# The recurrence over the context moved between the decays of later pieces, the later recurrence given precedence

## The chip, the cores and the metric

The kernel runs on one core of a Trainium2 chip. The metric is the device time of one launch in microseconds: for the kernel before, the median of 3 runs is 1711.6 (1711.44 to 1716.66). The engines are named as the profile does: PE (matrix products), PEld (loading of its weights), DVE (VectorE), ACT (ScalarE), POOL (GpSimd) and SP (the queue that issues the DMAs).

## The reference

One layer of a diffusion backbone, 1024 latent rows and 256 context rows of 1024 columns. Cut to what matters here:

```python
h  = modulate(rms_norm(x, norm1_g), shift, scale)        # the same for the context rows
cb, cc, cx, r, k, v, w_lo, a_lo, g_lo = split(h @ w_in)  # one input projection
def step(S, inp):                                        # a 64x64 state per head, 8 heads, two directions
    sa = einsum("bhvk,bhk->bhv", S, kk_t)
    S  = S * w_t - sa * b_t + v_t * k_t                  # w_t: the decay
    return S, einsum("bhvk,bhk->bhv", S, r_t)
ctx_state      = scan(step, zero, context rows)          # per direction
y              = scan(step, ctx_state, latent rows)      # starts from the context's last state
y_conv         = cb * shortconv1d(cc * cx, conv_a_w)
x = x + g1 * (concat(y_conv, rwkv_output(y, r, k, v, g_lo)) @ w_out)
x = x + g2 * conv_ffn(modulate(rms_norm(x, norm2_g), ...))   # gated, 3x3 convolution, 2816 columns
return rms_norm(x, final_g)
```

## The kernel before, in words

The recurrence is computed in chunks of 64 rows. Inside a chunk its rows form a triangular system; the kernel builds its matrices from the decays, inverts them, and then steps the state from chunk to chunk with matrix products. All of it is float32; wide products take their operands split in a high and a low part and are three products each.

**Stages, in the order of the program.** Modulation and norm; projections of k and v; then, for five *pieces* of 256 rows (one of the context, `ti` = 0, and four of the latents in the order 2, 8, 4, 6), `decay_and_invert(ti)`: `decays` (L524) makes decays and chunk matrices for four column groups `j` and two directions `d`, and `invert` (L652) inverts the piece's triangular blocks, mostly by 60 small products and sums on DVE (`tmp`, `ti`, L670 and L672). Beside the pieces stand `r_and_gate` (r and gate projections) and `conv_group` (the three projections of the short convolution and its arithmetic on DVE, L832 to L840); their products are `pj`, L354. In the text a *unit* is one column group of one piece, so 20 units; its end is the last reading of its chunk products `px` by DVE (L603).

**The steps.** `steps` (L723) advances both directions by one chunk. A step's chain is: `ry` (what the chunk's own rows and the state S give, L752 and L760, PE), `rh` (a copy, ACT for one direction and DVE for the other, L762), `pu` (L771, PE), `vu` (L775, L777), `ps` (L783, PE), the sum into S (L786, DVE), and then the next step's L760. POOL scales S (L764) and a chunk's `car` (L650). For the latents come the chunk's outputs: products L792 and their copy or sum (L800, L802). After every part of the chain `fill(n)` hands out n pieces of other work from a list (`pend`): the product of the convolution group with the output weights (`pco`), and from round 10 on mixing (`mix`), output product (`outp`, `po`) and the feed-forward's input (`to_h2`). The table SL says how many pieces stand in each of the four gaps of a round.

There are four steps over the context and then 16 *rounds* (r0 to r15) over the latents: r0 to r3 need the pieces 2 and 8 only, r4 is the first that needs piece 6. Before, the context's steps stand after all five pieces; behind each of them two of the eight blocks of `w_out` are multiplied by the gate (`w_make`, L891 on DVE, L892 on ACT, L893 on POOL), loaded two at a time.

**What sets the order.** A scheduler lists each engine's instructions, by priority in program order and by a model of time of its own; an engine then works through its list in that order. Tiles of SBUF and the eight PSUM banks are handed out by pools: a tile waits until the tile that held its place is done with. `B1` gives the banks for the pieces: `px` three, `pj` two, `pl` (decays' small products) two, `pq` one, and `ry`, `pu` one of `px`'s.

Of the kernel before, what the change touches and what calls it, by code (L numbers as in the profile page):

```python
# [2 lines left out]

# [12 lines left out]
D = 1024  # L16
# [6 lines left out]
CH = 64  # L23
# [5 lines left out]
TAIL = {10: "m3 m4", 11: "o3 o4 h3 h4", 12: "m2 m5", 13: "o2 o5 h2 h5", 14: "m1 m6", 15: "o1 o6 h1 h6", 16: "m0 m7", 17: "o0 o7", 18: "h0 h7"}  # L29
SL = ((3, 2, 0, 2),) * 10 + ((0, 1, 3, 4),) + ((4, 4, 4, 6),) * 5  # L30
RC = 9
# [3 lines left out]
YT = 2  # L35
IB = 2
XB, XT = 2, 3
PADC, PADM = 88, 80
PN1 = (5,)
NA = 17  # L40
XO = "xx0300301131x123222x"
AE = (0, 1, 0, 1, 0, 0, 1, 0)
B1 = ((4, 5, 1), (2, 3), (6, 7), (0,), (1,))
B2 = ((2, 3), (1, 6))
# [43 lines left out]
def hybrid_kernel(  # L88
# [96 lines left out]
    md = ss_.enter_context(tc.tile_pool(name="md", bufs=1, side="left", reuse_waits="tile"))  # L185
    md.tile([128, PADM], F32, name="padm")
    hsr = md.tile([128, 4, 2], F32, name="hsr")
# [325 lines left out]
    st = ss_.enter_context(tc.tile_pool(name="st", bufs=1, side="left", reuse_waits="tile"))  # L513
    sx = ExitStack()
    dq = sx.enter_context(tc.tile_pool(name="dq", bufs=2, side="left", reuse_waits="tile"))
    NP = 256
# [7 lines left out]
    def decays(pp, pieces):  # L524


        for ti in pieces:
# [4 lines left out]
            for j in range(4):  # L532
# [6 lines left out]
                if lat:  # L539
                    rt = dq.tile([128, NP], F32, name="dr")  # L540
                    SY.dma_start(rt, rd[j, :, t0 - CTX:t0 - CTX + n])
                    rk = dq.tile([128, NP], F32, name="rk", bufs=1)
                    G.tensor_tensor(out=rk, in0=rt, in1=k, op=ALU.mult)
                    pbn = pp.tile([128, 512], F32, name="pbn", tag="pl", bufs=2)
                    for q in range(2):
                        PE.matmul(pbn[:, 2 * q:2 * q + 2], rk[:, 128 * q:128 * q + 128], hsr[:, j, :], start=True, stop=True)
                    V.tensor_copy(bon[:, ti - 2:ti, 2 * j:2 * j + 2], pbn[:, 0:4].rearrange("p (t e) -> p t e", e=2))
# [70 lines left out]


    Sd = []  # L620
# [4 lines left out]
    zero = st.tile([128, 2], F32, name="zero")  # L625
    G.memset(zero, 0.0)
    yts, before = {}, [None, None]

    class Chunk:


        def __init__(self, pool, d, t, ch):
            self.d, self.t, self.ch, self.has_y = d, t, ch, t >= 2

            self.pc = before[d]
            before[d] = pcs[:, d, :, 2 * t + ch:2 * t + ch + 1]
            self.xa = pool.tile([128, 8, CH], F32, name="cxa")
            SY.dma_start(self.xa, xad[t // 2, :, ch, 2 * d + t % 2])
            self.kbt = pool.tile([128, 512], F32, name="ckb")
            SY.dma_start(self.kbt, kbd[d, t, ch])  # L640
            if self.has_y:
                self.ar = pool.tile([128, 4, 2 * CH], F32, name="car")
                SY.dma_start(self.ar, ard[d, t, ch])
                self.xr = pool.tile([128, 8, CH], F32, name="cxr")
                SY.dma_start(self.xr, xrd[d, t, ch])
            else:
                self.ar = pool.tile([128, 4, 2 * CH], F32, name="car")[:, :, 0:CH]
# [75 lines left out]
    def steps(pool, pairs, pp, bufs, sl=(0, 0, 0, 0)):  # L723


        cx = []
        rh = pool.tile([128, 512], F32, name="rh", bufs=1)
# [15 lines left out]
        rys = []  # L743
        for _ in cx:
            ry = pp.tile([128, 4, 128], F32, name="ry", tag="ry", bufs=bufs)
            rys.append((ry, ry.rearrange("p j (e v) -> p (j e) v", e=2)))
# [10 lines left out]
        for (u, v0, u0, vu, S), (ry, ry8) in both:  # L757
# [8 lines left out]
        pus = [pp.tile([128, 4, 128], F32, name="pu", tag="pu", bufs=bufs) for _ in cx]  # L766
        with turns():
# [4 lines left out]
        for (u, v0, u0, vu, S), pu in zip(cx, pus):  # L772
# [3 lines left out]
            else:  # L776
                chain["V"] = V.tensor_scalar(out=vu[u0:u0 + 64], in0=puf, scalar1=-1.0, scalar2=None, op0=ALU.mult)  # L777
        fill(sl[1])
        for u, v0, u0, vu, S in cx:

            ps = pp.tile([128, 4, 64], F32, name="ps", tag="pu", bufs=bufs)
            for h in range(8):
                chain["PE"] = PE.matmul(ps[64 * (h % 2):64 * (h % 2) + 64, h // 2, :], u.kbt[:, 64 * h:64 * h + 64], vu[:, 64 * h:64 * h + 64], start=True, stop=True)  # L783
            for e in range(2):
                r = slice(64 * e, 64 * e + 64)
                chain["V"] = V.tensor_tensor(out=S[r, :, r], in0=ps[r], in1=S[r, :, r], op=ALU.add)  # L786
        fill(sl[2])
        both = [z for z in both if z[0][0].has_y]
        with turns():
# [3 lines left out]
        for (u, v0, u0, vu, S), (ry, ry8) in both:  # L793
# [9 lines left out]
            e_[1] += 1  # L803
            if e_[1] == 2 and (first or t in (3, 4)):
                SY.dma_start(yd[t], e_[0])
        fill(sl[3])

# [36 lines left out]
    rg, cg = r_and_gate(), conv_group()  # L844

    def decay_and_invert(ti):
        for _ in decays(ppc, (ti,)):
            pass
        for _ in invert(ppc, ti):
            pass  # L850

    decay_and_invert(0)
    for _ in range(4):
        next(rg)
    for ti in (2, 8, 4, 6):
        decay_and_invert(ti)
# [11 lines left out]
    sh2 = ExitStack()  # L868
    h2p = sh2.enter_context(tc.tile_pool(name="h2p", bufs=1, side="left", reuse_waits="tile"))
    h2 = [[h2p.tile([128, 8, 512], F32R, name=f"h2{hf}{i}", tag=f"h2{hf}{i}") for i in range(2)] for hf in range(1)]  # L870

# [11 lines left out]
    def w_raw(k):  # L883
        raws_[k] = cp_.tile([128, D], F32, name="xo", bufs=XB)
        SY.dma_start(raws_[k], w_out[0, 128 * k:128 * k + 128, :])

    def w_make(k):
# [4 lines left out]
        A.copy(hl[0], raw)  # L892
        G.tensor_tensor(out=hl[1], in0=raw, in1=hl[0].bitcast(F32), op=ALU.subtract)  # L893

# [138 lines left out]
    stages = {"m": mix, "o": outp, "h": to_h2}  # L1033
    ppc = Banks(ry=B2[0], pu=B2[1])
    w_raw(0)
    w_raw(1)
    for r in range(4):
        steps(ring, [(0, r // 2, r % 2), (1, 1 - r // 2, 1 - r % 2)], ppc, 1)

        with behind():  # L1040
            w_make(2 * r)
            w_make(2 * r + 1)
        if r < 3:
            w_raw(2 * r + 2)
            w_raw(2 * r + 3)
        if r == 1:
            pend.append(conv_out())
            next(pend[0])
# [197 lines left out]
```

## Time and profile before

| | |
|---|---|
| median of 3 runs | 1711.6 us |
| the profiled execution | 1711.73 us, span 1710.0 us |
| PE busy | 1558.9 us (91%) |
| DVE busy | 1157.2 us (68%) |
| ACT, POOL busy | 565.1 (33%), 578.4 us (34%) |
| mean granted TensorE clock | 0.938 |

The busy share is an average over stages with different limits, so it is read stage by stage: which engine is busy there, and what ended its idle time. The pieces run from about 265 to 612 us, the context's steps from 617 us, the rounds until 938 us, the feed-forward from there to the end.

### The profile page before, as it was taken

Reading aid. Unit: us, or ns where it says so; the run is one execution under the profiler, and the core shown is the slowest. Engines: PE = TensorE matmul, PEld = TensorE weight load, DVE = VectorE, ACT = ScalarE, POOL = GpSimd, SP = SyncE. Lnnn points to the kernel's source line nnn. Section 1 sums busy time; section 2 is a strip of 40 time slices with the busy share of each in tenths; the row PEclk is TensorE's granted clock in tenths of the full one; section 3 lists DMA queues with packets and bytes.
Section 4 is the critical chain, followed back from the end, with each engine's and each line's share of the span. In section 5 each row is a group of like instructions: output and inputs, shape, how many; then the busy total and the mean of one; then the engine's idle time right before and its main releaser. Section 6 shows DMA issues by size and latency. Waiting matters only on the chain.

```text
span 1710.0 us, 27259 instructions
## 1 busy us (share of the span) xinstructions
PE 1558.9 (91%) x10639; PEld 1260.8 (74%) x10639; DVE 1157.2 (68%) x1795; ACT 565.1 (33%) x994; POOL 578.4 (34%) x515
## 2 busy tenths in 40 slices
PE   7699999989899966799678889999999999999997
PEld 2588768867777756687566768888888888788886
DVE  4963525698999987444578777777777777446645
ACT  2654315544445323221123421211111111324323
POOL 2343312333343304533344422222222222545643
PEclk9799799998999875999789999999999999999999
DMA  9385527557576486988652311111111111533531
GB/s 311 113 281 178 180 76 219 160 154 243 173 236 214 127 256 208 320 248 274 214 164 73 116 49 49 50 46 45 46 50 50 50 49 50 172 112 123 165 95 61
DMA packets 233721, 247.97 MB, mean 145 GB/s; under 512 B 18547, under 2 KB 171720, under 8 KB 233592
## 3 DMA queue, kind: packets, MB, share of 16 engines
q1 hardware_dynamic: 233208, 246.07, 46.2%
q8 instruction: 84, 1.38, 0.3%
q14 instruction: 45, 0.37, 0.1%
q0 software_dynamic: 384, 0.15, 0.0%
HBM read 179.32 MB, written 66.85 MB: 144 GB/s over the span
## 4 chain that ended last, share of the span: by engine, by line
PE 64%; DVE 23%; DMA 6%; ACT 3%; issue 3%; SPq 1%; POOL 0%; DVEq 0%; ACTq 0%
PE pf L1099 26%; PE pf L1179 13%; PE pj L354 10%; DVE tmp L670 3%; DVE ti L672 3%; PE pco L898 2%; PE po L898 2%; DMA araw<-in_ada_w_dram 2%; DVE acc L1146 2%; PE ry L760 1%; DVE xrO L605 1%; PE ry L752 1%; DVE xa L603 1%; PE ps L783 1%; PE px L601 1%
## 5 line engine op out<-in xcount | busy, mean ns | idle before, releaser
L1099 PE MATMUL pf<-h,fhi 128*128 128x512 f32 x1408 | 385.9, 391 | 5.9 <-DVE act L1151 4.1
L1099 PEld LDWEIGHTS pf<-h,fhi 128*128 128x128 f32 x1408 | 265.7, 189 | 62.6 <-DVE act L1151 4.5
L354 PE MATMUL pj<-hx,whi 128*128 128x512 f32 (+1 forms) x976 | 302.5, 389 | 1.6 <-DVE hx L328 1.3
L1146 DVE SCALAR_TENSOR_TENSOR acc<-gp,prm,acc 128x1024 f32<-128x1024 f32 x176 | 273.0, 1553 | 6.0
L106 POOL TENSOR_TENSOR flo<-fraw,fhi 128x1024 fp32r<-128x1024 f32 x50 | 122.0, 2441 | 315.8 <-ACT fhi L105 315.8
L1099 PE MATMUL pf<-h,flo 128*128 128x512 f32 x704 | 224.9, 392 | 0.0
L354 PEld LDWEIGHTS pj<-hx,whi 128*128 128x128 f32 x976 | 184.6, 197 | 38.2 <-issue 4.4
L354 PE MATMUL pj<-hx,wlo 128*128 128x512 f32 (+1 forms) x488 | 189.5, 389 | 0.0
L1179 PE MATMUL pf<-dhi,ahl 128*128 128x512 f32 x640 | 163.0, 389 | 0.2 <-DVE ahl L1171 0.2
L1171 DVE TENSOR_TENSOR ahl<-act,ahl 128x512 fp32r<-128x512 f32 x44 | 86.2, 1969 | 101.5 <-ACT ahl L1170 101.5
L1099 PEld LDWEIGHTS pf<-h,flo 128*128 128x128 f32 x704 | 132.9, 189 | 27.7 <-POOL flo L106 0.2
L105 ACT CAST fhi<-fraw 128x1024 fp32r<-128x1024 f32 x50 | 52.6, 1053 | 265.8 <-issue 158.4
L1179 PEld LDWEIGHTS pf<-dhi,ahl 128*128 128x128 f32 x640 | 120.0, 188 | 25.5 <-DVE ahl L1171 0.6
L106 POOL TENSOR_TENSOR dlo<-fraw,dhi 128x1024 fp32r<-128x1024 f32 x40 | 98.5, 2467 | 93.7 <-ACT dhi L105 89.7
L106 POOL TENSOR_TENSOR wlo<-wraw,whi 128x1024 fp32r<-128x1024 f32 x26 | 63.2, 2431 | 165.1 <-ACT whi L105 165.0
L1144 DVE TENSOR_SCALAR acc<-gp,prm 128x1024 f32<-128x1024 f32 x22 | 42.6, 1938 | 98.2 <-ACT gp L1136 98.2
L354 PEld LDWEIGHTS pj<-hx,wlo 128*128 128x128 f32 x488 | 96.2, 197 | 17.3 <-issue 1.7
L1179 PE MATMUL pf<-dlo,ahl 128*128 128x512 f32 x320 | 89.1, 389 | 0.0
L601 PE MATMUL px<-arO,kbO 64*128 64x128 f32 (+1 forms) x640 | 64.1, 308 | 18.3 <-DVE xrO L605 12.5
L601 PEld LDWEIGHTS px<-arO,kbO 64*128 64x128 f32 x640 | 51.9, 206 | 35.1 <-issue 29.2
L105 ACT CAST dhi<-fraw 128x1024 fp32r<-128x1024 f32 x40 | 41.9, 1050 | 105.0 <-PE pf L1179 87.5
L764 POOL TENSOR_TENSOR S<-S,pcs 128x512 f32<-128x512 f32 x38 | 40.1, 1069 | 94.1 <-PE ry L760 93.9
(281 smaller groups left out, 2621.6 us busy)
## 6 DMA issues: line engine op xcount, KB each, us to landing
araw<-in_ada_w_dram SPq DMA_DIRECT2D x48, 512.0 KB, 5.5
fraw<-in_ffn_w_up_dram SPq DMA_DIRECT2D x46, 512.0 KB, 3.9
fraw<-in_ffn_w_down_dram SPq DMA_DIRECT2D x44, 512.0 KB, 3.7
wraw<-in_w_in_dram SPq DMA_DIRECT2D x26, 512.0 KB, 5.3
lu<-lu_dram SPq DMA_DIRECT2D x20, 512.0 KB, 5.3
kb_dram<-kbT SPq DMA_DIRECT2D x40, 256.0 KB, 3.1
xa_dram<-xa SPq DMA_DIRECT2D x20, 512.0 KB, 4.9
cxa<-xa_dram SPq DMA_DIRECT2D x40, 256.0 KB, 3.8
```

The lines of the kernel that those rows point to most:

```text
L105: A.copy(hi, src)
L106: G.tensor_tensor(out=lo, in0=src, in1=hi.bitcast(F32), op=ALU.subtract)
L354: PE.matmul(p[:, :n], w[:, k, :], hsl(i, k, t0, n), start=(k == 0 and first), stop=(k == 7 and last))
L601: PE.matmul(px[:, ch, i, 0:w], kbO[r, i, 2 * ch:2 * ch + 2, :].rearrange("p s n -> p (s n)"), rhs, start=True, stop=True)
L670: V.tensor_tensor(out=tv, in0=ti[:, j + 1:32, j:j + 1].to_broadcast([128, m, j]), in1=ti[:, j:j + 1, 0:j].to_broadcast([128, m, j]), op=AL ...
L672: V.tensor_tensor(out=ti[:, j + 1:32, 0:j], in0=ti[:, j + 1:32, 0:j], in1=tv, op=ALU.add)
L898: m = PE.matmul(po, hl[:, a_, k, :], w[k][b_][:, sl], start=(k == 0 and f), stop=(k == 3 and l))
L1099: PE.matmul(pts[hf], w[:, k, :], h2[hf][i_][:, k, :], start=(k == 0 and f), stop=(k == 7 and l))
L1144: V.tensor_scalar(out=acc, in0=src, scalar1=wcol, scalar2=prm[:, P_FB + f:P_FB + f + 1], op0=ALU.mult, op1=ALU.add)
L1146: V.scalar_tensor_tensor(out=acc, in0=src, scalar=wcol, in1=acc, op0=ALU.mult, op1=ALU.add)
L1171: V.tensor_tensor(out=hl[:, 1, :], in0=asl, in1=hl[:, 0, :].bitcast(F32), op=ALU.subtract)
L1179: PE.matmul(pd[i], hl[:, a_, 128 * q:128 * q + 128], w[w_][:, 512 * nh:512 * nh + 512], start=(f == 0 and s_), stop=(f == NF - 1 and l_))
```

## The change

The four context steps are issued inside the loops of the pieces 2 and 8: `decay_and_invert` calls `steps` at the yields 5 and 13 of a piece (`CS`), with tiles from a pool of their own (`rc`, two buffers) and PSUM bank 7, which is taken from `pl`. To make room, the inversion's tiles, `dr` and the tile of `rk` (now `db`'s) lose their second buffer. All instructions of the steps get a priority 400 places earlier (`HP`). The eight blocks of `w_out` are loaded at once, into tiles of the later stage; `w_make` stands behind the rounds r0 to r3 instead of behind the context's steps. The rounds r0 and r1 hand out no other work, r2 to r8 eight pieces instead of seven. The output tiles of the latent tiles 3 and 4 stay in SBUF until they are mixed, and are no longer written out and read back.

```diff
-SL = ((3, 2, 0, 2),) * 10 + ((0, 1, 3, 4),) + ((4, 4, 4, 6),) * 5
+SL = ((0, 0, 0, 0),) * 2 + ((4, 2, 0, 2),) * 7 + ((4, 4, 0, 4),) + ((0, 1, 3, 4),) + ((4, 4, 4, 6),) * 5
-IB = 2
+IB = 1
+CS = (5, 13)
+HP = 400
-B1 = ((4, 5, 1), (2, 3), (6, 7), (0,), (1,))
+B1 = ((4, 5, 1), (2, 3), (6,), (0,), (7,))
...
+    rc = sx.enter_context(tc.tile_pool(name="rc", bufs=2, side="left", reuse_waits="tile"))
...
-                    rt = dq.tile([128, NP], F32, name="dr")
+                    rt = dq.tile([128, NP], F32, name="dr", bufs=1)
...
-                    rk = dq.tile([128, NP], F32, name="rk", bufs=1)
+                    rk = dq.tile([128, NP], F32, name="rk", tag="db", bufs=1)
...
     def steps(pool, pairs, pp, bufs, sl=(0, 0, 0, 0)):
+        hp = ExitStack()
+        hp.enter_context(tc.high_priority(offset=HP))
...
+        hp.close()
         fill(sl[0])
+        hp.enter_context(tc.high_priority(offset=HP))
...
-            if e_[1] == 2 and (first or t in (3, 4)):
+            if e_[1] == 2 and first:
                 SY.dma_start(yd[t], e_[0])
...
+    before_y = []
+
     def decay_and_invert(ti):
-        for _ in decays(ppc, (ti,)):
-            pass
-        for _ in invert(ppc, ti):
-            pass
+        for n, _ in enumerate(chainit(decays(ppc, (ti,)), invert(ppc, ti))):
+            if n in CS and before_y:
+                steps(rc, before_y.pop(0), ppc, 1)

     decay_and_invert(0)
     for _ in range(4):
         next(rg)
+    before_y += [[(0, r // 2, r % 2), (1, 1 - r // 2, 1 - r % 2)] for r in range(4)]
...
     def w_raw(k):
-        raws_[k] = cp_.tile([128, D], F32, name="xo", bufs=XB)
+        raws_[k] = [x2s[1][:, 2], x2s[1][:, 3], X2[1], X2[6], X2[2], X2[5], None, None][k]
+        if k > 5:
+            raws_[k] = cp_.tile([128, D], F32, name="xo", bufs=XB)
...
     def mix_load(t):
         y = yts[t, False][0]
-        if t in (3, 4):
-            y = op.tile([128, 512], F32, name="y", bufs=NY)
-            SY.dma_start(y, yd[t])
...
-    ppc = Banks(ry=B2[0], pu=B2[1])
-    w_raw(0)
-    w_raw(1)
-    for r in range(4):
-        steps(ring, [(0, r // 2, r % 2), (1, 1 - r // 2, 1 - r % 2)], ppc, 1)
-
-        with behind():
-            w_make(2 * r)
-            w_make(2 * r + 1)
...
+    for k in range(8):
+        w_raw(k)
...
     for r in range(16):
...
         steps(ring, [(0, 2 + r // 2, r % 2), (1, 9 - r // 2, 1 - r % 2)], pp, 2, SL[r])
+        if r < 4:
+            with behind():
+                w_make(2 * r)
+                w_make(2 * r + 1)
```

The order of the instructions moves far more than the context's steps. PE's list, before, in the last piece (`px`: chunk products, `pj`: projection products, `pt`: transposes, `plo`: decays' small products):

```order
L354 MATMUL pj<-hx,whi 128x512
L601 MATMUL px<-arO,kbO 128x128
L354 MATMUL pj<-hx,whi 128x512
L354 MATMUL pj<-hx,wlo 128x512
L354 MATMUL pj<-hx,whi 128x512 x2
L601 MATMUL px<-arO,kbO 128x128 x7
L609 MATMUL pt<-cst,kbO 128x128 x4
L555 MATMUL plo<-dxl,lu 128x256
L556 MATMUL plo<-dxl,lu 128x256
```

The same place of the changed program (its lines are four further on: L605 is `px`, L613 `pt`, L559 and L560 `plo`, L550 `pbn`):

```order
L605 MATMUL px<-arO,kbO 128x128 x8
L613 MATMUL pt<-cst,kbO 128x128 x4
L605 MATMUL px<-arO,kbO 128x128
L550 MATMUL pbn<-hsr,rk 128x2 x2
L613 MATMUL pt<-cst,kbO 128x128 x4
L605 MATMUL px<-arO,kbO 128x128 x7
L559 MATMUL plo<-dxl,lu 128x256
L560 MATMUL plo<-dxl,lu 128x256
```

No projection product is left there. Counted over PE's list by unit, from the end of unit 1 on: before, the units 2 to 20 hold 32, 32, 32, 60, 39, 46, 12, 59, 37, 48, 8, 53, 39, 37, 35, 45, 40, 43 and 22 of them; now the units 2 to 10 hold 62, 62, 65, 117, 87, 80, 81, 86 and 63, and the units 11 to 20 none (16 more stand in unit 1).

On DVE, at the end of the last inversion (`xa` is its last copy), the list before goes on with a step of the context. Now the context is long done, r0 and r1 stand inside the inversion, and this is r2 and r3, with the eight products of `w_make` (L915 is the old L891) behind r3's `vu`:

```order
L685 COPY xa<-xr 32x32x32 x2
L769 COPY rh<-ry 64x512
L940 TENSOR_TENSOR chl<-chl 128x512
L788 TENSOR_SCALAR vu<-pu 64x512
L940 TENSOR_TENSOR chl<-chl 128x512
L801 TENSOR_TENSOR S_2053<-ps,S_2053 64x4x64 x2
L801 TENSOR_TENSOR S_2055<-ps,S_2055 64x4x64 x2
L769 COPY rh<-ry 64x512
L788 TENSOR_SCALAR vu<-pu 64x512
L915 TENSOR_TENSOR x_6989<-x_6989,gb_6993 128x1024
L801 TENSOR_TENSOR S_2053<-ps,S_2053 64x4x64 x2
L915 TENSOR_TENSOR x_6989<-x_6989,gb_6993 128x1024 x2
```

On PE in the later rounds, before: the outputs of a round (L792) and the next round's first products (L752) stand behind output products `po` (L898):

```order
L792 MATMUL ry<-vu,cxr 64x64
L981 MATMUL py<-cst,y 128x128 x4
L792 MATMUL ry<-vu,cxr 64x64 x8
L898 MATMUL po<-wh_6942,chl 128x512
L898 MATMUL po<-wl_6943,chl 128x512
L898 MATMUL po<-wh_6942,chl 128x512
L898 MATMUL po<-wl_6943,chl 128x512
L752 MATMUL ry<-vu,cxa 64x64
L898 MATMUL po<-wh_6942,chl 128x512
```

Now (L782 is `pu`, L798 `ps`, L809 the outputs, L924 `po`) a round's chain stands whole, and `po` mostly behind it:

```order
L782 MATMUL pu<-rh,cxa 64x64 x15
L1004 MATMUL py<-cst,y 128x128 x4
L924 MATMUL po<-wh_7612,chl 128x512
L924 MATMUL po<-wl_7613,chl 128x512
L924 MATMUL po<-wh_7612,chl 128x512
L924 MATMUL po<-wh_7618,chl 128x512
L924 MATMUL po<-wl_7619,chl 128x512
L924 MATMUL po<-wh_7618,chl 128x512
L798 MATMUL ps<-vu,ckb 64x64 x8
L809 MATMUL ry<-vu,cxr 64x64
L798 MATMUL ps<-vu,ckb 64x64 x8
L809 MATMUL ry<-vu,cxr 64x64 x15
```

Behind them stand 24 products `po` in a row; over the rounds 96 of the 192 come after the last round, before some 72.

## Rows read from the trace of the kernel before

**Rows 1.** Busy time of the engines in six stretches

```profile
core 0: us, PE busy (x) PEld busy (x) DVE busy (x) ACT busy (x) POOL busy (x), PEclk, DMA share, GB/s
284.50:323.40 38.90, 38.90 (x253) 31.60 (x252) 20.91 (x42) 17.44 (x35) 12.67 (x20) 1.00 0.55 169
323.40:612.20 288.80, 262.69 (x2299) 213.36 (x2299) 274.71 (x639) 137.19 (x258) 99.42 (x151) 0.93 0.61 185
612.20:683.00 70.80, 43.60 (x845) 39.36 (x841) 52.75 (x95) 22.40 (x31) 22.23 (x18) 0.59 0.82 254
683.00:808.00 125.00, 114.42 (x1706) 95.12 (x1703) 57.05 (x94) 28.25 (x47) 53.34 (x46) 0.97 0.89 281
808.00:938.80 130.80, 98.16 (x1086) 78.78 (x1087) 87.99 (x174) 37.12 (x88) 50.44 (x50) 0.87 0.49 153
938.80:1030.00 91.20, 80.87 (x355) 64.75 (x354) 68.89 (x98) 30.79 (x66) 30.33 (x22) 0.96 0.26 82
```

**Rows 2.** Chain of waits, round r2 and its successor: start, us, engine, tile, line

```profile
718.17 0.90 PE ry L752 x26
...
721.23 2.06 PE pco L898 x9
...
727.15 0.87 PE ry L792 x29
...
729.61 0.90 PE ry L752 x26
```

**Rows 3.** DVE by line, 323.4 to 612.2 us: the convolution group's arithmetic

```profile
L836 DVE SCALAR_TENSOR_TENSOR cy<-cu,prm,cy 128x1024 f32<-128x1024 f32 x8 | 10.6, 1329 | 0.0
...
L832 DVE TENSOR_TENSOR cu<-pj,cu 128x512 f32<-128x512 f32 x8 | 5.5, 682 | 0.0
L840 DVE TENSOR_TENSOR cy<-pj,cy 128x512 f32<-128x512 f32 x8 | 5.4, 679 | 0.0
L834 DVE TENSOR_SCALAR cy<-cu,prm 128x1024 f32<-128x1024 f32 x4 | 5.1, 1270 | 0.0
```

**Rows 4.** DVE in time: ends of units 11 and 12 (start, us, engine, line, operation)

```profile
461.06 0.41 DVE L603 TENSOR_TENSOR xa<-px,cst 128x256 f32<-128x256 f32 x1
...
468.25 0.42 DVE L603 TENSOR_TENSOR xa<-px,cst 128x256 f32<-128x256 f32 x1
```

**Rows 5.** PE in time: half of the first products of an inversion

```profile
606.20 1.20 PE L688 MATMUL pq<-rti,xa 32*32 32x32 f32 x64 [0.91 <-DVE rti L678]
```

**Rows 6.** DVE in time: the last inversion, and a step's work behind it

```profile
612.58 1.39 DVE L660 COPY xb<-xa 32x1024 f32<-32x1024 f32 x2
616.68 1.92 DVE L664 STREAM_TRANSPOSE ti<-xb 128x1024 f32<-128x1024 f32 x1 [2.72 <-ACT xb L660]
618.68 0.17 DVE L670 TENSOR_TENSOR tmp<-ti 128x30 f32<-128x30 f32 x1
...
628.31 0.41 DVE L672 TENSOR_TENSOR ti<-ti,tmp 128x238 f32<-128x238 f32 x1
...
659.01 1.94 DVE L676 STREAM_TRANSPOSE xr<-ti 128x1024 f32<-128x1024 f32 x1
...
664.44 1.40 DVE L681 COPY xa<-xr 32x1024 f32<-32x1024 f32 x2
...
670.69 0.68 DVE L777 TENSOR_SCALAR vu<-pu 64x512 f32<-64x512 f32 x1 [4.13 <-PE pu L771]
675.13 1.75 DVE L786 TENSOR_TENSOR S<-ps,S 64x256 f32<-64x256 f32 x4 [3.76 <-PE ps L783]
```

**Rows 7.** The weights' products on DVE: least, median, greatest ns

```profile
L891 DVE TENSOR_TENSOR xo<-xo,gb x8: 1217/1224/1735, 638.6 to 702.7; 128x1024 f32<-128x1024 f32 x8
```

**Rows 8.** PE in time: first products of rounds r10 and r11

```profile
808.02 0.33 PE L752 MATMUL ry<-vu,cxa 64*64 64x64 f32 x2 [1.16 <-DVE yt L802]
...
827.65 0.47 PE L752 MATMUL ry<-vu,cxa 64*64 64x64 f32 x2 [9.90 <-DVE y L802]
```

**Rows 9.** DVE in time: what it waited for between them

```profile
821.89 0.69 DVE L959 TENSOR_REDUCE mu<-y 128x8 f32<-128x512 f32 x1 [5.85 <-DMA y<-y_dram]
```

More of the change, by code (lines that the diff above doesn't have):

```diff
@@ L2 @@
 from contextlib import ExitStack, contextmanager
+from itertools import chain as chainit
 import concourse.bass as bass
@@ L35 @@
 YT = 2
-IB = 2
+IB = 1
 XB, XT = 2, 3
-PADC, PADM = 88, 80
+CS = (5, 13)
+HP = 400
+PADC, PADM, PADS = 88, 80, 8
 PN1 = (5,)
@@ L185, in hybrid_kernel @@
     md = ss_.enter_context(tc.tile_pool(name="md", bufs=1, side="left", reuse_waits="tile"))
-    md.tile([128, PADM], F32, name="padm")
     hsr = md.tile([128, 4, 2], F32, name="hsr")
@@ L617, in decays @@
                 yield
+    st.tile([128, PADS], F32, name="pads")
     Sd = []
@@ L624, in hybrid_kernel @@
         Sd.append(S0)
-    zero = st.tile([128, 2], F32, name="zero")
-    G.memset(zero, 0.0)
+    zero = rst.rearrange("p (b t) -> p b t", t=CH)[:, 0:2, 0]
     yts, before = {}, [None, None]
@@ L646, in __init__ @@
             else:
-                self.ar = pool.tile([128, 4, 2 * CH], F32, name="car")[:, :, 0:CH]
+                self.ar = pool.tile([128, 4, CH], F32, name="car")
                 SY.dma_start(self.ar, arc[d, t, :, :, ch, :])
@@ L743, in steps @@
         rys = []
-        for _ in cx:
-            ry = pp.tile([128, 4, 128], F32, name="ry", tag="ry", bufs=bufs)
+        for u, *_ in cx:
+            if u.has_y or not rys:
+                ry = pp.tile([128, 4, 128], F32, name="ry", tag="ry", bufs=bufs)
             rys.append((ry, ry.rearrange("p j (e v) -> p (j e) v", e=2)))
@@ L764, in steps @@
                 chain["G"] = F2.tensor_tensor(out=S, in0=S, in1=u.pc.to_broadcast([128, 4, 128]), op=ALU.mult)
+        hp.close()
         fill(sl[0])
-        pus = [pp.tile([128, 4, 128], F32, name="pu", tag="pu", bufs=bufs) for _ in cx]
+        hp.enter_context(tc.high_priority(offset=HP))
+        pus = []
+        for u, *_ in cx:
+            pus.append(pp.tile([128, 4, 128], F32, name="pu", tag="pu", bufs=bufs) if u.has_y or not pus else pus[0])
         with turns():
@@ L777, in steps @@
                 chain["V"] = V.tensor_scalar(out=vu[u0:u0 + 64], in0=puf, scalar1=-1.0, scalar2=None, op0=ALU.mult)
+        hp.close()
         fill(sl[1])
+        hp.enter_context(tc.high_priority(offset=HP))
         for u, v0, u0, vu, S in cx:
-            ps = pp.tile([128, 4, 64], F32, name="ps", tag="pu", bufs=bufs)
+            if u.has_y or u.d == 0:
+                ps2 = pp.tile([128, 2, 4, 64], F32, name="ps", tag="pu", bufs=bufs)
+            ps = ps2[:, u.d]
             for h in range(8):
@@ L786, in steps @@
                 chain["V"] = V.tensor_tensor(out=S[r, :, r], in0=ps[r], in1=S[r, :, r], op=ALU.add)
+        hp.close()
         fill(sl[2])
+        hp.enter_context(tc.high_priority(offset=HP))
         both = [z for z in both if z[0][0].has_y]
@@ L803, in steps @@
             e_[1] += 1
-            if e_[1] == 2 and (first or t in (3, 4)):
+            if e_[1] == 2 and first:
                 SY.dma_start(yd[t], e_[0])
+        hp.close()
         fill(sl[3])
@@ L869, in hybrid_kernel @@
     h2p = sh2.enter_context(tc.tile_pool(name="h2p", bufs=1, side="left", reuse_waits="tile"))
+    h2p.tile([128, PADM], F32, name="padm")
     h2 = [[h2p.tile([128, 8, 512], F32R, name=f"h2{hf}{i}", tag=f"h2{hf}{i}") for i in range(2)] for hf in range(1)]
@@ L892, in w_make @@
         A.copy(hl[0], raw)
-        G.tensor_tensor(out=hl[1], in0=raw, in1=hl[0].bitcast(F32), op=ALU.subtract)
+        for i in range(2):
+            c = slice(512 * i, 512 * i + 512)
+            G.tensor_tensor(out=hl[1][:, c], in0=raw[:, c], in1=hl[0][:, c].bitcast(F32), op=ALU.subtract)
     def product(po, hl, w, sl):
@@ L1033, in hybrid_kernel @@
     stages = {"m": mix, "o": outp, "h": to_h2}
-    ppc = Banks(ry=B2[0], pu=B2[1])
-    w_raw(0)
-    w_raw(1)
-    for r in range(4):
-        steps(ring, [(0, r // 2, r % 2), (1, 1 - r // 2, 1 - r % 2)], ppc, 1)
-        with behind():
-            w_make(2 * r)
-            w_make(2 * r + 1)
[L1043 to L1048, printed above, removed]
+    for k in range(8):
+        w_raw(k)
+    pend.append(conv_out())
+    next(pend[0])
     plan = dict(TAIL)
```

## The prediction

> **What bounds the kernel now.** I read the busy time by stretch first, because the 91% of PE on the page is an average over stages with different limits. Four stretches matter. In units 2 to 4 PE is busy all of the 38.9 us and DVE half of them; in the units 5 to 20 (323.4 to 612.2) DVE is busy 274.7 of 288.8 us, 95%, and PE 262.7; PE and DVE are both nearly full there [rows 1]. From 612.2 to 683.0, where the last inversion and the context's steps run, nobody is full: PE 43.6 of 70.8 us at a granted clock of 0.59, DVE 52.8. From 683 to 808 (r0 to r9) PE is full but for one wait. From 808.0 to 938.8 (r10 to r15) DVE has 88.0 us of work in 130.8 [rows 1], and one wait stands out: PE does nothing for 9.90 us at 827.65, because DVE in its order sits until 821.89 on an output tile that was written out and is read back [rows 8, 9]. So a change can win in the third and the last stretch, and must not lose in the second, where the work of two engines just fits one beside the other.
>
> **What the change does to the pieces: a loss.** The moved steps are the small part. By the counts of the order, of the 719 projection products of units 2 to 20, 703 now stand in units 2 to 10 (16 moved into unit 1), and none in 11 to 20. PE is then the limit of the first half, and DVE that of the second, one after the other instead of together.
>
> First half, PE: a projection product takes 2.06/9 = 0.229 us in a row [rows 2], so 703 take 161.0 us. The decays' own products of a unit: units 2 to 4 take 38.9 us with 96 projection products, so (38.9 - 22.0)/3 = 5.6 us; nine units 50.6 us, and 2 us more since six of them, unlike those three, are latent ones with wider `px`. One inversion and three quarters: four groups of products of 1.20 us each [rows 5], 8.4 us. Four context steps: a round takes 729.61 - 718.17 = 11.44 us with 21 products `pco`, so its own chain is 11.44 - 4.81 = 6.6 us of PE, without the outputs' 0.87 some 5.7 us [rows 2]; four are 22.8 us. Sum 244.8 us. Where DVE has an inversion and the convolution's arithmetic in one unit (5 and 9) it has 2 or 3 us more to do than PE: 5 us.
>
> Second half, DVE: the four latent pieces take 288.8/4 = 72.2 us each, of which (10.6 + 5.5 + 5.4 + 5.1)/4 = 6.6 is the convolution's arithmetic [rows 1, 3], which now stands in the first half. Two pieces without it: 131.2 us. Units 11 and 12, with neither inversion nor convolution: unit 12 took 468.67 - 461.47 = 7.2 us [rows 4], units 2 to 4 13.0; I take 9 us, nearest to unit 12, so 18. Sum 149.2 us.
>
> With the 16 products in unit 1 (3.7 us), units 2 to 20 take 244.8 + 5 + 149.2 + 3.7 = 402.7 us instead of 612.2 - 284.5 = 327.7: 75 us later. The single buffers (`pl`, `dr`, `rk` with `db`, the inversion) show nowhere in this trace. In the first half PE's queue hides them; in the second each may cost the column groups that have no inversion beside them something between 0 and the 5.8 us by which units 2 to 4 are longer than unit 12, for six such units at most 35 us. I add 5 for them and for waits in the steps' chains, near the lower end, since DVE's order has other work in most units: **80 us of loss**, between 68 and 105. The steps' 32 loads and 12 POOL operations hide: POOL is busy 99 of 288.8 us and the DMA engines 61% [rows 1].
>
> One row speaks for the upper end: in 612.2 to 683.0, where PE is busy 43.6 of 70.8 us, the granted clock is 0.59, so that it was at 1.2 GHz most of the time, and in 284.5 to 323.4, where it never stops, 1.00 [rows 1]. The Trainium skill says the same (TensorE: Matmul & The Clock Gate, What's actually happening): the half rate is the default, and work releases it. It makes the second half's sparse PE a candidate for the half rate; by it alone the ten units' own 56 us of products would be 112, still under DVE's 149, so the sum would not change and the chains behind one another would get longer. This is the second rival.
>
> **From the last chunk products to round r10: a gain.** Before: 808.0 - 612.2 = 195.8 us. Now the context is gone from it, and r0 and r1 run inside the last inversion, as `pu` of r0 waits only for the decays' banks. By DVE's order: block copies, wait for ACT and transpose as now, 612.58 to 618.6, 6 us; 30 pairs of products and sums, 628.7 - 618.7 = 10 us for the first 15 [rows 6], so some 21; the steps' own DVE work, two sums of 1.75 into S, two `vu` of 0.68 and a copy `rh` as long, 5.5; two transposes of 1.94 and the last copy of 1.40, 5.3 [rows 6]. Before, the same stretch from 618.7 to 659.0 took 40.3 us for some 30 us of such work, the rest being waits and slower operations; I take half of that, 6. Sum 44. Then r2 without other work, 9 us (between the 6.6 of PE's own chain and the 11.44 of a full round), and r3 with the eight products of 1.22 us [rows 7] in the way of the next `rh`: 18. After 71 us r4 has its `rh`, and PE is fed with `pco`: r4 to r9 hold 6 x 6.6 + 184 x 0.229 = 81.7 us of PE work, of which 3 are done by then. r10 starts 71 + 79 = 150 us after the last chunk products: **46 us of gain**, between 38 (all waits as before) and 57 (none). The weights' loads, issued at once, have this whole stretch; that hides them unless they delay the chunks' loads in SP's queue.
>
> **The rounds r10 to r15: a gain.** The read-back goes, and with it 9.9 us of PE's wait. What is late next is DVE's own work: 88 us in the stretch. Before, it filled 67% of it, in the pieces 95%. With the chain's instructions ahead I take 87%, between the two: 101 us instead of 130.8, 30 us of gain; floor 88, and 121 if only the read-back goes. Against it stand 24 output products (5.5 us of PE) that now come after the last round. The stretch behind it has 10.3 us without PE [rows 1], so I charge 3: **27 us of gain**, between 7 and 40.
>
> **Sum.** 80 - 46 - 27 = 7 us slower than the profiled 1711.7, which is the median: 1719.
>
> **The rivals.** *Even or faster by the chain* (the other side): the rounds are short because the chain stands first. For it: the wait of 9.90 us certainly ends, and DVE's 88 us is far below 130.8. Against: mixing needs ACT's root and POOL's products between DVE's own, in the same order, so DVE waits for others there. Its place is 808 to 1030; its price, with DVE at its floor and the tail's 10 us gone, 43 + 10 = 53 us instead of 27; from 34 us on the kernel is not slower, from 39 measurably faster. Time 1711.7 + 80 - 46 - 53 = 1693, and 1703 with half of it. *The second half at half clock*: chunk products, inversions and the last steps take twice as long in a chain with single buffers; of the 56 us some 25 come on the path: 1744. *The change does not move the start of the rounds*: the last inversion ends as late as before after the last chunk products (53.6 us to its last copy [rows 6], not 44) and r0 to r3 only run behind it, some 20 us more: 1739. For it, that r4 needs it anyway; against, that r0 and r1 stand between its operations in the order.
>
> **How the numbers follow.** Forecast, with its own range from 1707 to 1731: 0.5. Faster by the chain: 0.24. Half clock: 0.15. Rounds no earlier: 0.11. Four terms with 10 us of doubt or so each give some 20 us together, so the range that should hold the time 8 times in 10 is 1694 to 1748. What can be told from no change is 0.3%, 5 us: faster by more than that has all but 0.02 of the second case and 0.06 of the forecast, 0.28; within it the forecast's lower part and the rest, 0.20; slower 0.52.
>
> **What would show it.** In the profile after: PE 95% busy and DVE below 80% up to the end of unit 10, some 538 us; then DVE full and PE below half, no `pj` at all, until the last chunk products at some 692 us instead of 612. Granted clock in that stretch: above 0.8 for the forecast, near 0.5 for the half clock. r10 begins some 150 us after the last chunk products, and r10 to r15 take about 100 us, with no wait for a read-back. The prediction is wrong if the last chunk products come before 670 us (then PE's or DVE's work was overcounted), or if the rounds take over 120 us.

## The result, and the profile after

The changed kernel takes 1798.0 us (1795.8 to 1803.9) against 1711.5 (1710.3 to 1716.7): a ratio of 1.0506, 95% interval 1.0484 to 1.0527. Forecast were 1719 us (1694 to 1748). The profiled execution has a span of 1801.7 us, 91.7 more than before.

The busy time by stretch, which answers to [rows 1]. The columns are window, length, busy time of PE, PEld, DVE, ACT and POOL with their counts, granted clock, DMA share, GB/s:

```profile
285.40:537.50 252.10, 241.57 (x2060) 197.59 (x2060) 175.47 (x363) 96.16 (x167) 74.63 (x95) 0.97 0.52 154
537.50:737.10 199.60, 122.10 (x1152) 99.31 (x1144) 148.26 (x352) 74.22 (x148) 54.50 (x95) 0.56 0.60 187
737.10:810.60 73.50, 42.02 (x803) 37.14 (x801) 49.77 (x97) 21.70 (x33) 16.54 (x14) 0.66 0.58 186
810.60:910.60 100.00, 91.93 (x1076) 74.88 (x1075) 44.24 (x65) 21.09 (x32) 47.87 (x39) 0.92 0.73 232
910.60:1021.50 110.90, 86.60 (x1046) 71.41 (x1046) 85.60 (x168) 32.44 (x78) 48.48 (x45) 0.86 0.52 167
```

The stretches are units 2 to 10, units 11 to 20, from the last chunk products to round r4, r4 to r9, and r10 to r15. The first came out as forecast: unit 10 ends at 537.5 us, PE busy 96%, DVE 70%. The second did not. DVE's work in it is 148.3 us, as forecast, but it takes 199.6: PE is at 61% with a granted clock of 0.56, and nobody is full. Units 11 and 12, 7.2 us apart before [rows 4], end 18.9 us apart, DVE in time:

```profile
556.68 0.42 DVE L607 TENSOR_TENSOR xa<-px,cst 128x256 f32<-128x256 f32 x1
...
575.62 0.42 DVE L607 TENSOR_TENSOR xa<-px,cst 128x256 f32<-128x256 f32 x1
```

What DVE waited for in that stretch (engine, line, releaser: us in total, times, longest):

```profile
DVE bon L551 <- PE pbn L550: 13.1, 5, 5.0
DVE sw L566 <- ACT sw L563: 12.9, 5, 3.8
DVE xa L607 <- PE px L605: 11.9, 6, 2.4
DVE db L583 <- ACT da L563: 4.7, 5, 2.6
```

Before, from 300 us to the end of the pieces, so in units 3 to 20, the same four waits were

```profile
DVE xa L603 <- PE px L601: 13.8, 6, 4.8
DVE bon L547 <- PE pbn L546: 2.9, 1, 2.9
DVE db L579 <- ACT da L559: 2.5, 2, 1.4
DVE sw L562 <- ACT sw L559: 1.2, 1, 1.2
```

and here is one such wait in time, between units 11 and 12, all engines (in brackets the idle time before and what ended it):

```profile
554.76 0.62 SPq L545 DMA_DIRECT2D dr<-r_dram  x1
...
557.02 0.42 DVE L609 TENSOR_TENSOR xrO<-px,cst 128x256 f32<-128x256 f32 x1
...
560.66 0.72 POOL L547 TENSOR_TENSOR rk<-dr,dk 128x256 f32<-128x256 f32 x1 [8.51 <-issue]
561.43 1.01 PE L550 MATMUL pbn<-hsr,rk 128*128 128x2 f32 x4 [4.03 <-POOL rk L547]
562.48 0.16 DVE L551 COPY bon<-pbn 128x4 f32<-128x4 f32 x1 [5.05 <-PE pbn L550]
562.70 0.58 PE L559 MATMUL plo<-dxl,lu 128*128 128x256 f32 x1 [0.25 <-DVE bon L551]
...
563.53 0.47 ACT L563 ACTIVATE sw<-plo,prm 128x256 f32<-128x256 f32 x1 [5.49 <-PE plo L560]
564.04 0.29 DVE L566 TENSOR_SCALAR sw<-sw 128x256 f32<-128x256 f32 x1 [1.39 <-ACT sw L563]
...
564.06 0.58 PE L559 MATMUL plo<-dxl,lu 128*128 128x256 f32 x1 [0.56 <-ACT sw L563]
```

`dr` has one buffer, so its load for unit 12 is issued at 554.76; `rk` needs it (and `dk`, whose load, issued just before in the same queue, landed at 558.98); `pbn` needs `rk`; `bon` must empty the only bank of `pl` before `plo` may write it; and the next `plo` waits until ACT has read that bank. Four engines stand in one line, and DVE does nothing from 557.4 to 562.5.

Where DVE's idle time of the second stretch lies, by pairs of units (11 and 12, 13 and 14, and so on to 20):

```profile
537.50:576.00 38.50, 22.29 (x174) 17.43 (x166) 20.63 (x47) 11.82 (x26) 9.04 (x19) 0.57 0.85 276
576.00:614.90 38.90, 22.04 (x110) 17.18 (x108) 37.80 (x94) 13.80 (x27) 12.64 (x22) 0.54 0.66 191
614.90:655.30 40.40, 27.17 (x362) 22.91 (x362) 24.94 (x62) 17.17 (x34) 7.80 (x18) 0.54 0.60 189
655.30:707.10 51.80, 26.08 (x196) 21.18 (x197) 45.27 (x110) 17.32 (x32) 17.22 (x22) 0.60 0.41 123
707.10:737.10 30.00, 24.52 (x324) 20.61 (x318) 19.62 (x44) 14.11 (x30) 7.80 (x15) 0.50 0.55 172
```

In units 13 and 14, where an inversion's work stands in DVE's list, DVE is idle for 1.1 us of 38.9. Of its 51.3 idle us 43.7 lie in the first, third and last pair, where there is no inversion or only the end of one.

The last chunk products end at 737.1 us, 124.9 later than before. From there to r10 it is 173.5 us instead of 195.8, r10 to r15 take 110.9 instead of 130.8, and the rest 780.2 instead of 771.2: 124.9 - 22.3 - 19.9 + 9.0 = 91.7.

### The profile page after: what moved, and what is told of

Read it like the earlier page. It is cut to its first block, busy times and chain, and to the rows that moved or that the text cites. A ratio compares the mean times of both kernels' runs of the same rounds, so it can differ in the third digit from the quotient of the medians.

```text
span 1801.7 us, 27158 instructions
## 1 busy us (share of the span) xinstructions
PE 1597.9 (89%) x10639; PEld 1292.4 (72%) x10639; DVE 1167.6 (65%) x1795; ACT 571.0 (32%) x994; POOL 589.1 (33%) x522
## 4 chain that ended last, share of the span: by engine, by line
PE 43%; DVE 6%; DMA 1%; issue 1%; ACT 1%; POOL 0%; SPq 0%; DVEq 0%; ACTq 0%
PE pf L1115 25%; PE pf L1195 11%; PE pco L924 2%; PE po L924 2%; DVE acc L1162 1%; PE ry L767 1%; PE ry L759 1%; PE pu L782 0%; PE ps L798 0%; DVE S L801 0%; DVE rstd L177 0%; DVE acc L1160 0%; DMA lng<-in_rw_ln_g_dram 0%; DVE rstd L178 0%; DMA fraw<-in_ffn_w_down_dram 0%
## 5 line engine op out<-in xcount | busy, mean ns | idle before, releaser
L356 PE MATMUL pj<-hx,whi 128*128 128x512 f32 (+1 forms) x976 | 297.2, 385 | 1.3 <-DVE hx L330 0.9
L109 POOL TENSOR_TENSOR dlo<-fraw,dhi 128x1024 fp32r<-128x1024 f32 x40 | 98.3, 2465 | 92.4 <-ACT dhi L108 91.7
L605 PE MATMUL px<-arO,kbO 64*128 64x128 f32 (+1 forms) x640 | 68.5, 361 | 27.1 <-DVE kbO L587 14.2
L576 POOL COPY pcs<-P 128x4 f32<-128x4 f32 x40 | 12.9, 323 | 230.5 <-ACT P L574 230.5
L771 POOL TENSOR_TENSOR S<-S,pcs 128x512 f32<-128x512 f32 x38 | 40.8, 1082 | 143.9 <-PE ry L767 120.7
L605 PEld LDWEIGHTS px<-arO,kbO 64*128 64x128 f32 x640 | 58.5, 256 | 37.2 <-issue 35.4
```

The lines of the kernel that those rows point to most:

```text
L109: G.tensor_tensor(out=lo, in0=src, in1=hi.bitcast(F32), op=ALU.subtract)
L356: PE.matmul(p[:, :n], w[:, k, :], hsl(i, k, t0, n), start=(k == 0 and first), stop=(k == 7 and last))
L605: PE.matmul(px[:, ch, i, 0:w], kbO[r, i, 2 * ch:2 * ch + 2, :].rearrange("p s n -> p (s n)"), rhs, start=True, stop=True)
```

## The experiments

"Last px" is where DVE begins its last reading of chunk products in the profiled execution (612.2 before, 737.1 in the changed kernel). It is one execution each, and the two of one kernel, y_kept and y_kept_again, differ by 5 us in it. The ratio is against the kernel before, timed beside the run.

| kernel | us | ratio, interval | last px |
|---|---|---|---|
| buf_only | 1804.8 | 1.0536 (1.0512-1.0559) | 712.6 |
| pl_only | 1792.9 | 1.0462 (1.0438-1.0485) | 699.6 |
| sbuf_only | 1750.1 | 1.0207 (1.0180-1.0234) | 657.6 |
| spread | 1829.4 | 1.0685 (1.0654-1.0715) | 749.1 |
| warm | 1815.7 | 1.0604 (1.0587-1.0620) | 734.1 |
| rk_own | 1802.9 | 1.0523 (1.0502-1.0545) | 712.6 |
| pl_two | 1764.4 | 1.0301 (1.0276-1.0325) | 695.8 |
| pl_two_pj | 1723.4 | 1.0060 (1.0040-1.0080) | 657.4 |
| best_hpctx | 1728.2 | 1.0075 (1.0049-1.0101) | 633.4 |
| best_hp0 | 1721.8 | 1.0042 (1.0027-1.0057) | 637.8 |
| late_only | 1726.3 | 1.0073 (1.0045-1.0102) | 610.6 |
| late_nohp | 1710.8 | 0.9989 (0.9971-1.0006) | 613.8 |
| late_w2 | 1712.9 | 1.0000 (0.9985-1.0014) | 611.0 |
| hp_only | 1720.7 | 1.0043 (1.0026-1.0059) | 613.4 |
| y_kept | 1701.5 | 0.9927 (0.9899-0.9955) | 614.1 |
| y_kept_again | 1700.0 | 0.9916 (0.9900-0.9932) | 608.9 |

**The buffers alone (buf_only).** The kernel before with

```diff
-IB = 2
+IB = 1
-B1 = ((4, 5, 1), (2, 3), (6, 7), (0,), (1,))
+B1 = ((4, 5, 1), (2, 3), (6,), (0,), (7,))
-                    rt = dq.tile([128, NP], F32, name="dr")
+                    rt = dq.tile([128, NP], F32, name="dr", bufs=1)
-                    rk = dq.tile([128, NP], F32, name="rk", bufs=1)
+                    rk = dq.tile([128, NP], F32, name="rk", tag="db", bufs=1)
```

> The kernel before with the changed kernel's buffers and banks alone (one bank for pl, one buffer for the inversion's tiles and dr, rk in db's tile, ry and pu in bank 7); no step is moved, and everything after the pieces is as before. Theory A (the cut buffers let the scheduler drain the projections into the first half, and the second half then runs as bare chains): the projections stand in units 2 to 10 here too, the last chunk products come at 737 less the four steps' 23 us of PE, some 712 us instead of 612, and the time is near 1811 us (1795 to 1825). Theory B (the moved steps, with their loads and their precedence, hold up the pieces' queues): at most 1725 us, last chunk products before 630.

Measured: 1804.8 us, last px 712.6. Theory B falls. Without one step moved the loss is there, and a little larger than the whole change's. The projections move forward too: in the trace all of those behind unit 1 stand in units 2 to 9, none in 10 to 20.

**Which buffer (pl_only, sbuf_only).** The second line pair of that diff alone, and the other three alone.

> The kernel before with one bank instead of two for pl (ry and pu in bank 7), nothing else. Theory C (the single bank makes each column group a chain: product, ACT's tanh, next product, and DVE waits for both): it carries nearly the whole loss of the four cut buffers, 1790 us (1775 to 1808), and DVE waits for the tanh 40 us or more in the pieces, against 4 before. Rival D (the SBUF buffers carry it: dr's load is waited for by rk, pbn and everything behind pbn on PE): below 1755.

> The kernel before with the cuts in SBUF alone: one buffer for the inversion's tiles and for dr, rk in db's tile; pl keeps its two banks. Theory C: 1728 us (1715 to 1745): by the order the projections end with unit 16, the last four units run bare, but the tanh is not waited for. Rival D: 1760 or more, with PE waiting for rk and pbn.

Measured: 80 us and 38 us, together more than the 91 of both, so they overlap. The bank alone loses most, as theory C said; the cuts in SBUF lose more than I expected and less than rival D. With one bank alone the projections end with unit 10, with the cuts in SBUF alone with unit 15. DVE's waits for the tanh in the pieces of pl_only, over the 40 us that theory C gave (1.2 and 2.5 before):

```profile
DVE sw L562 <- ACT sw L559: 24.9, 14, 3.2
DVE db L579 <- ACT da L559: 21.5, 14, 4.3
```

and PE's in those of sbuf_only, where `rk` stands in `db`'s tile and waits for its last reader:

```profile
PE pbn L546 <- POOL rk L543: 11.9, 6, 4.1
PE plo L555 <- DVE bon L547: 7.4, 3, 3.6
```

**The order or the buffers (spread).** In all buffers the changed kernel, with the projections forced back among the units:

```diff
+        edge = ExitStack()
+        if gate:
+            edge.enter_context(tc.issue_after(pxi[gate.pop(0)].ins))
         for (t0, n), p in zip(segs, pts):
...
+        edge.close()
...
+    gate += [8, 10, 12, 14, 16, 20, 22, 24, 26, 30, 32, 34, 36]
```

(`pxi` holds the last chunk product of each half unit, `gate` the half unit that a projection is queued behind.)

> The changed kernel, all its buffers, banks and moved steps kept, with one addition: each of the 13 projections of the gate and the convolution group is queued on PE behind the chunk products of one of the units 5 to 19, so that every unit again holds some 35 of their products. Theory A (the loss is the order: no filler beside the chains of the second half): the pieces need about 286 us of PE, last chunk products near 640, time 1705 us (1690 to 1730). Theory C (the single buffers themselves make the chains of each unit longer, whatever PE does meanwhile): last chunk products still after 700, time above 1760 us.

Measured: 1829.4 us. Theory A, which was mine until here, falls: with filler in nearly every unit the pieces are slower still. PE waits on the same chain, in the pieces of spread:

```profile
PE px L610 <- DVE kbO L591: 28.3, 11, 8.2
PE plo L563 <- ACT da L567: 22.8, 14, 7.0
PE plo L563 <- ACT sw L567: 16.0, 16, 2.3
```

Before, no `plo` waited for `da`, and for `sw` 0.2 us. The forced order makes waits of its own, though: DVE waited 15.2 us for projection products here. So spread shows that filler alone does not bring the time back, not what a better order with single buffers would take. Together with buf_only and pl_only, where the projections move forward with no step moved, I read the early projections as a symptom: the single buffers hold the chain up, the scheduler fills the gaps with projections, and when these are used up the gaps stay empty.

**The clock (warm).** 32 transposes of a constant behind the small products of each half unit from unit 11 on:

```diff
+    for m in warm:
+        with tc.issue_after(m.ins):
+            pw = ppc.tile([128, 512], F32, name="pw", tag="pj", bufs=2)
+            for i in range(32):
+                PE.transpose(pw[:, 128 * (i % 4):128 * (i % 4) + 128], ident, ident)
```

> The changed kernel with 32 extra transposes of a constant on PE behind the small products of each of the 20 half units of units 11 to 20 (640 in all, into pj's free banks; they add work and change no result). At 0.107 us each at full clock they are 68 us of PE in a stretch of 200 us in which PE was busy some 115 at a granted clock of 0.55. Theory G (the half clock lies on the path there, since chunk products, small products and transposes stand in a chain with DVE and ACT): the clock rises above 0.85 and the last chunk products come 20 us or more before 737; time 1775 us or less. Theory H (the chain's waits are ACT's and DVE's, PE's clock does not matter): clock up, but time 1795 to 1805.

Measured: 1815.7 us. The granted clock of the stretch rose from 0.56 to 0.87, and the last px came 3 us earlier:

```profile
537.50:734.10 196.60, 155.31 (x1748) 142.18 (x1744) 142.37 (x351) 74.23 (x146) 44.69 (x91) 0.87 0.60 185
```

That is nearer to theory H than to G, but 3 us is a net figure, and from one execution each. The transposes stand in PE's list among the chain's products, and in 9 of 20 places the chunk products begin right behind them, as here, where their last input was ready at 686.4:

```profile
687.16 1.49 PE L887 MATMUL pw<-cst 128*128 128x128 f32 x10
688.59 1.16 PE L607 MATMUL px<-arO,kbO 64*128 64x128 f32 x16
```

What the clock alone costs in the pieces is therefore not measured. That the whole became 17 us longer was in neither theory. It arises behind the rounds: r15's outputs are ready 12 us earlier than in the changed kernel, but the last output product starts 12 us later (1083.6 against 1071.2).

**The second tie (rk_own).** `rk` and `dr` with buffers as before, one staging buffer less (`STG` 2 for 3), `pl` still single.

> The changed kernel with pl's single bank, but with a tile of its own for rk and two buffers for dr again (room from one staging buffer less, 2 instead of 3). In the changed kernel PE waited 15.5 us for rk between 540 and 737, and the next column group's small products stood behind that. Theory M (the two ties, pl's bank and rk in db's tile, lie in one chain; with one loosened the other still holds it): 1785 to 1796. Theory N (they add up: the cuts in SBUF cost 38 of 91 us, most of it by rk): 1770 or less.

Measured: 1802.9 us, neither theory. But its last px comes 24.5 us earlier than in the changed kernel, so this tie does count in the pieces. The gain is lost at the end: r15's outputs are ready 29 us earlier (992 against 1021), the last output product starts at 1069.8 against 1071.2, and PE waits between:

```profile
PE ph L1038 <- DVE xt L1026: 11.9, 2, 8.3
PE ph L1038 <- ACT h L1046: 5.8, 4, 1.7
```

In the changed kernel these waits are 2.8 us from 1000 us on. From the start of the last output product to the end it is 727 to 731 us in all the traces of this case, before and after too: what happens ahead of that product counts only as far as it moves it.

**The bank given back (pl_two, pl_two_pj).** The changed kernel with

```diff
-B1 = ((4, 5, 1), (2, 3), (6,), (0,), (7,))
+B1 = ((4, 5, 1), (2, 3), (6, 7), (0,), (1,))
```

and, in pl_two_pj, `((4, 5, 1), (2,), (6, 3), (0,), (7,))` instead.

> The changed kernel with pl's second PSUM bank given back (ry and pu of the context share a bank of px, as before). By the order the projections then reach into unit 14 instead of ending with unit 10. Theory A: the bare second half shrinks from ten units to six, last chunk products near 700, time 1760 us (1735 to 1775). Theory B (moved steps): as the changed kernel, 1798 us, or worse, since the steps now share a bank with px. Theory C: better than 1760 only if pl is the buffer that costs.

> The changed kernel with two banks for pl again, the second one taken from pj (which keeps one); the context's steps stay in the pieces, in their own bank 7. By the order every unit to the last holds 48 to 96 projection products per two units again. Theory C (pl's bank is the loss, the moved steps themselves cost their 23 us of PE and no more): last chunk products near 645, 1735 us (1712 to 1755). Rival B (the moved steps' waits hold up the pieces): 1764 or more, as with the bank taken from px. If one bank for pj costs instead, PE waits for the projections' copies, and it shows there.

Measured: 1764.4 us, inside theory A's range, and 1723.4, inside theory C's. With the bank taken from `pj`, 75 of the 86 us are gone and the moved steps are all still there. The pieces are 45 us longer than before; the steps' 23 us of PE and the cuts in SBUF (45 us by the last px of sbuf_only) are in it, and no run parts them. The projections stand in every unit again here, so this run alone does not tell bank from filler. In pl_two they end with unit 13; the units 14 to 20, with two banks and no projection, take 128 us against 140 in the changed kernel and 118 before. Why pl_two, whose steps share a bank with `px`, is 41 us slower than pl_two_pj was not traced further.

**The later part (late_only, hp_only, y_kept, late_nohp, late_w2).** late_only is the changed kernel with the steps behind the pieces and the pieces' buffers as before; hp_only and y_kept are the kernel before with one edit each, the precedence and

```diff
-            if e_[1] == 2 and (first or t in (3, 4)):
+            if e_[1] == 2 and first:
...
-        if t in (3, 4):
-            y = op.tile([128, 512], F32, name="y", bufs=NY)
-            SY.dma_start(y, yd[t])
```

> The changed kernel with the context's four steps put back behind the pieces and all buffers and banks of the pieces as before; what stays is the precedence of the steps' instructions, the weights loaded at once, w_make behind r0 to r3, SL, and the tiles that are not written out and read back. Theory A: pieces as before, last chunk products at 612; rounds r10 to r15 110.9 instead of 130.8 us as in the changed kernel, 9 us of that given back behind them: 1701 us (1690 to 1712). If the shorter rounds came only from the context being done early, 1711 or more.

> The kernel before with one edit: all instructions of the steps get a priority 400 places earlier. The read-back stays. Theory I (precedence makes the last rounds shorter, and the output products that it pushes behind the last round cost as much): 1709 to 1720 us, r10 to r15 some 115 instead of 130.8, the stretch behind them longer by as much. Theory J (precedence is a gain of its own): below 1705 us. Theory K (it is what makes the later changes alone 13 us slower): 1720 or more.

> The kernel before with one edit: the output tiles 3 and 4 are not written out and read back. Theory E (the read-back was a wait of 9.9 us on the path): 1703 us (1699 to 1707). Rival F (what the later rounds win is given back behind them, since the feed-forward waits for the mixing and output products of the last tiles all the same): 1709 to 1716, no change.

> The later changes alone (1726.3 us) without the precedence: steps behind the pieces, all buffers as before, weights loaded at once, w_make behind r0 to r3, the changed SL, tiles 3 and 4 not written out and read back. Theory K (the precedence costs): near 1703 us, as with the tiles kept alone (1701.5). Theory L (weights at once, w_make in the rounds and SL cost: the first step waited 14.1 us for vu in all, behind the weights' loads): 1718 us or more.

Measured: the tiles kept gain 11 us, all of the read-back's wait (theory E). The precedence alone loses 8, at the border of theories I and K. Late_only, of which I expected 1701, loses 13, though its six rounds are short (107.1 us). Without the precedence (late_nohp) the same kernel takes 15.5 us less and is level with the one before, between theories K and L. In hp_only r10 to r15 take 109.2 us, 22 less than before, and the rest takes 804.6, 33 more. Its windows, the six rounds and the 82.4 us behind them, and y_kept's:

```profile
808.40:917.60 109.20, 82.97 (x1034) 67.63 (x1034) 75.46 (x156) 30.49 (x73) 43.35 (x42) 0.87 0.59 181
917.60:1000.00 82.40, 60.70 (x249) 46.43 (x250) 48.02 (x90) 26.69 (x64) 29.50 (x24) 0.80 0.22 73
```

```profile
812.10:928.30 116.20, 90.69 (x1060) 74.47 (x1061) 86.05 (x168) 35.08 (x83) 55.07 (x49) 0.87 0.52 163
928.30:1010.70 82.40, 76.89 (x343) 61.24 (x342) 58.20 (x90) 31.20 (x69) 28.35 (x21) 0.98 0.28 87
```

With precedence DVE has done 75 us of work in the rounds instead of 88 [rows 1]: part of the mixing is left for later (16 of its 32 transposes stand behind r15, 8 before), and there PE is busy 74% instead of y_kept's 93%. It waits for a tile's norm, in hp_only, and neither before nor in y_kept:

```profile
PE ph L1025 <- DVE xt L1013: 11.2, 2, 7.6
```

> The later changes alone without precedence (1710.8 us), with one edit: the weights are loaded two at a time behind each of the context's four steps again, instead of all eight at once ahead of them. There PE waited 24.7 us for vu's load between 612 and 823, against 3.8 us with the tiles kept alone. Theory P (the 4 MB stand ahead of the steps' loads in SP's queue, and that is the 9 us): 1701 us (1696 to 1705), wait for vu below 6 us. Theory Q (w_make behind r0 to r3 and the changed SL cost it): 1708 to 1713, whatever the wait is.

Late_w2 loads the weights two at a time behind the context's steps. Measured: 1712.9 us. It doesn't decide: six of the eight loads were still issued in a row (probably since their tiles lie where the pieces' tiles were; this was not traced),

```profile
669.28 4.26 SPq L908 DMA_DIRECT2D x<-in_w_out_dram  x6
```

and PE still waited 23.0 us for `vu`, against 3.8 in y_kept. What the 9 us between late_nohp and y_kept are stays open.

**Versions to beat both (best_hpctx, best_hp0, y_kept_again).** pl_two_pj with `rk` and `dr` as in rk_own, and the precedence for the context's steps only (`offset=HP if pool is rc else 0`), or `HP = 0`.

> The changed kernel with two banks for pl (the second from pj), rk with a tile of its own and two buffers for dr (two staging buffers instead of three), and the precedence for the context's steps only, not for the rounds. From the runs: 1723.4 with pl's banks alone, less the 15.5 us between the later changes with and without the precedence, less some 5 us for rk: 1703 us (1693 to 1715). Theory O (precedence in the rounds is only harmful where the context's steps stand behind the pieces, since r0 to r3 come late there): 1715 or more.

> The same without precedence for the context's steps too. If the moved steps need it (they stand in DVE's and PE's order among the pieces' work, and r0 waits for the last of them): 8 us or more above the kernel with the precedence for the context. If not: within 5 us of it.

> The kernel before with the tiles 3 and 4 kept, the same as before, timed in more rounds and on the chip of the run above: 1701.5 us again (1699 to 1705), ratio 0.993.

Measured: 1728.2, 1721.8 and 1700.0 us. The first is a miss by 25 us: its last px comes 24 us earlier than pl_two_pj's, but 72 projection products now stand behind the last unit, and r10 begins 5 us later (833 against 828). The time is one that theory O gave, but these products are another cause for it, so O is not shown. The moved steps don't need precedence: without it the kernel takes no longer (6 us less). The best kernel is the one before with the two tiles kept, 0.84% faster (0.68 to 1.00%).

## Why the prediction was wrong

**Units 2 to 10: right.** 538 us was forecast for the end of unit 10, 537.5 measured. That it fits to half a microsecond is luck: the stretch began 2.8 us earlier than added up and took 2.3 us longer.

**Units 11 to 20: wrong, and this is most of it.** The step that failed is "I add 5 for them and for waits in the steps' chains", for the single buffers. It was 50 us: 199.6 instead of 149.2. DVE's work was sized right (148.3); that DVE would be full was the mistake. I bounded the buffers by 5.8 us for each of six units that have nothing beside them, 35 us at most, and chose near the lower end because "DVE's order has other work in most units". Where it has an inversion that held, as units 13 and 14 show. The price of a bare unit did not: DVE idles 17.9 us in units 11 and 12 alone, 9 us each, and 43.7 in the six units 11, 12, 15, 16, 19 and 20. I had taken the price from units 2 to 4, which have both banks and a full PE and, as units of the context, no `rk` and `bon` at all. The runs show that the buffers are the cause: buf_only, pl_only and sbuf_only have the loss without the steps, pl_two_pj has the steps and 75 us less of the loss. How much of the 50 us is a wait for a buffer, and how much the empty PE beside it, is not parted. Neither of the two signs of being wrong that I had named came up (the last px came at 737, not before 670, and the rounds took 111 us, not over 120): for the pieces I had looked only for a loss counted too high.

More deeply, I took the moved projections as a cause, and built both halves on it. That the scheduler moved 703 products forward was, I now think, the sign that its model already saw the chain stall: in buf_only it does so with no step moved, and in spread putting them back by force does not help.

**The half clock: there, but not shown to cost much.** I named 0.5 against 0.8 as the sign, and 0.56 came. In warm a clock of 0.87, bought with transposes that stand in the chain's way, gives 3 us back. In spread the clock is 0.80 from 500 us, the end of unit 10, to the last px, and that takes 249 us. A rival can show its mark in the profile and still not be what costs most.

**From the last px to r10: 22 us of gain instead of 46.** Until r4 it went nearly as worked out: the last copy of the inversion ended 40.8 us after the last px (44 forecast), r4's first products came after 73.5 (its `rh` was forecast after 71):

```profile
776.47 1.41 DVE L685 COPY xa<-xr 32x1024 f32<-32x1024 f32 x2
```

R4 to r9 then took 100 us, not 79: 82 us of PE at full-clock rows became 91.9 at a granted clock of 0.92, and the rest is waits, 3.6 us for the weights' low parts on POOL and 3.3 for DVE. The first `pco`, just ahead of r4, had waited 10.6 us for `wh`.

**R10 to r15: 20 us of gain instead of 30, and 9 given back instead of 3.** The read-back's 9.9 us [rows 8, 9] was right, and y_kept has it in full. The error was to expect more from the precedence. Alone it loses 8 us: the rounds get shorter in part by the mixing that they leave for later, and the output products and the feed-forward wait for that.

**The moved steps: about right.** Their 23 us of PE were charged; the changed kernel's last px comes 24.5 us after that of buf_only, which moves none. No run moves them without the cuts. Whole change less buf_only, all the rest of it together is a gain of 7 us.

## What to carry to other kernels

A second buffer that shows no wait in a trace is not free to take: it may be why there is none. Before cutting one, follow a tile from writer to last reader across the engines and add up the round trip; here product, tanh, next product, four times a unit. When a planner moves a lot of other work forward after such a cut, take that as a possible sign of the stall, and try the cut alone before pricing the rest.

A stretch that gets shorter is a gain only if what follows it was waiting for it: look at the first operation behind it that is on the path, here the last output product, before crediting the difference.

## What the hardware showed

Raising PE's granted clock from 0.56 to 0.87 over 200 us by work of no use brought the end of the stretch 3 us forward, net of what that work held up. And two losses in one stretch overlap: one PSUM bank instead of two cost 80 us, the cuts in SBUF 38, both together 91.
